# Weights, low weights and activations put at other places in the on-chip memory, and another order in the mixers' matmul triples

## The chip, the cores and the metric

The kernel runs on one core of a Trainium2 chip. The metric is the device time of one execution in microseconds (us). Data is worked on in an on-chip memory of 128 partitions; a tile of shape [128, n] of 4-byte numbers takes 4n bytes of each partition, and its place is the byte in the partition at which it starts.

## The reference

Two blocks of a network on x of 256 tokens by 1024 features. The first block has two layers (a convolution mixer, then neighbourhood attention over x and a context of 256 tokens), the second two layers (a gated linear-attention mixer A, then a sliding-window attention mixer B, each with heads that read a memory of 256 tokens), with gated feed-forward networks (FFNs) before and behind each mixer. Cut to the parts that cost most:

```
def _swiglu(h, w_in, w_out):
    gate, up = jnp.split(h @ w_in, 2, axis=-1)
    return (jax.nn.silu(gate) * up) @ w_out

# first block, each layer
h = _modulate(_rms_norm(x, norm_mix[i]), sh1, sc1)
y = mixer(h)                    # convolution, or attention
x = x + g1 * y
x = x + g2 * _swiglu(_modulate(_rms_norm(x, norm_ffn[i]), sh2, sc2), ffn_w_in[i], ffn_w_out[i])
# second block, each layer
x = x + 0.5 * swiglu(rms_norm(x, ffn1_norm_g[i]), ffn1_w_in[i], ffn1_w_out[i])
proj = rms_norm(x, mix_norm_g[i]) @ w_in
x = x + concatenate([heads(proj), memory_heads(proj)]) @ w_out
x = x + 0.5 * swiglu(rms_norm(x, ffn2_norm_g[i]), ffn2_w_in[i], ffn2_w_out[i])
```

The features are 1024, the hidden width of an FFN 2816, all in 32-bit floats.

## The kernel before

Everything is kept transposed: features in the partitions (8 blocks of 128), tokens along the row. To keep precision in TensorE's fast 32-bit format, each number is split into a high part and a low part (its rest), and a product of two numbers is three matmuls: high by high, high by low, low by high.

Weights come from memory through `WeightStream`: SP's queue loads units of 1024 columns into `wraw` (five buffers), ScalarE copies the high part to `whi` (line 106), VectorE subtracts to get `wlo` (line 107), four buffers each, two units ahead of their use. The order of the units is written out by hand in `stream_specs`.

A matmul has an operand that is loaded into TensorE beforehand (its own LDWEIGHTS instruction; I say "the loaded operand") and one that is streamed through it (the moving operand), 256 or 512 columns wide. There are these forms:

- `mm3` (lines 246 to 248): a triple for one block of 128 features. `wstat` loads weights and streams activations; `xstat` and `xstat_steps` load activations and stream weights. In a triple the loaded operands are high, high, low and the moving ones high, low, high. The convolution and the first FFN's input stream 512 columns (x beside the context), nearly all else 256.
- `pair_unit` (lines 309 and 311), used by `ffn_pairs` for the five other FFNs: the activations' high plane and low plane lie side by side in `x2` (or `s2`, the hidden layer), so one matmul of 512 columns with the high weights does two products; the low weights then take the high plane alone, 256 columns. Four (at unit ends two) of the first kind are followed by as many of the second. `pg` is the accumulator of an FFN's input half, `po` that of its output half.

The order of the work around is that of the program; in attention and the mixers two strands are woven by estimated costs (`weave`).

Where a tile lies follows from the sizes of the tiles opened before it, pool by pool from the left end of the partition, and from the right end for a few. Nothing else sets it: several tiles of before have no use but to shift others (`fill3` to `fill11`, the argument `shift` of `ffn2`, the odd lengths and offsets in `x_tiles`, `net.xc` and `net.xa`).

Of the kernel before, what the change touches and what calls it, by code (L numbers as in the profile page):

```python
# [7 lines left out]
F32 = mybir.dt.float32  # L8
F32R = mybir.dt.float32r
# [6 lines left out]
P = 128  # L16
D = 1024
KB = D // P
T = 256
# [47 lines left out]
class WeightStream:  # L67
# [4 lines left out]
    def __init__(self, net, es, specs, raw_bufs, split_bufs, ahead):  # L72
        self.nc = net.nc
        self.specs = specs
        self.ahead = ahead
        self.raw_bufs = raw_bufs
        self.raw_pool = es.enter_context(net.tc.tile_pool(name="wraw", bufs=raw_bufs))
        self.split_pool = es.enter_context(net.tc.tile_pool(name="wsplit", bufs=split_bufs))
        self.loaded = 0
        self.split = 0  # L80
        self.used = 0
        self.raw = []
        self.ready = []
        self.width = 512
# [9 lines left out]
    def _split(self):  # L94
        self.load(self.split + self.raw_bufs)
        raw, nk, ncol = self.raw.pop(0)
        n = nk * ncol
        v = lambda t: t[:, :n].rearrange("p (k c) -> p k c", k=nk)
        if self.specs[self.split][3]:
            self.ready.append((v(raw), None, nk, ncol))  # L100
        else:
            hi = self.split_pool.tile([P, self.UNIT], F32R, name="whi", tag="hi")
            lo = self.split_pool.tile([P, self.UNIT], F32R, name="wlo", tag="lo")
# [58 lines left out]
class Net:  # L162
    def __init__(self, tc, a, out, es):
        self.tc = tc
        self.nc = tc.nc
        self.a = a
        self.out = out
        self.es = es
        nc = self.nc
# [23 lines left out]
    def x_tiles(self):  # L193

        return [self.xp.tile([P, KB * 512 + n], F32R, name=name, tag=name) for name, n in (("xh", 48), ("xl", 80))]

# [47 lines left out]
    def mm3(self, ps, ah, al, bh, bl, first, last):  # L244
        mm = self.nc.tensor.matmul
        mm(ps, ah, bh, start=first, stop=False)  # L246
        mm(ps, ah, bl, start=False, stop=False)  # L247
        mm(ps, al, bh, start=False, stop=last)  # L248
# [24 lines left out]

    def wstat(self, pss, xh, xl, kblocks):

        done = 0
        while done < len(kblocks):
            unit = self.ws.take()
            self.wstat_unit(unit, pss, xh, xl, kblocks, done)
            done += unit[2]  # L280

    def wstat_unit(self, unit, pss, xh, xl, kblocks, done):
# [32 lines left out]

    def xstat(self, bank, xh, xl):
        for _ in self.xstat_steps(bank, range(2), xh, xl, self.take2()):
            pass

    def partial(self, kblocks, yh, yl, evac, bank=None):  # L320
# [447 lines left out]
def conv_block(net):  # L768
# [134 lines left out]
    with tc.tile_pool(name="hid0", bufs=1) as hp, tc.tile_pool(name="ada", bufs=2) as net.adap:  # L903
        sh = hp.tile([P, 12, 512], F32R, name="sh")
        sl = hp.tile([P, 12, 512], F32R, name="sl")
        evict(0, 2)
# [120 lines left out]
def attention_block(net):  # L1027
# [6 lines left out]
    with ExitStack() as es:  # L1034
        op = es.enter_context(tc.tile_pool(name="attn1", bufs=1))
        heads_pool = es.enter_context(ExitStack())
        ap = heads_pool.enter_context(tc.tile_pool(name="attn", bufs=2))
        oh = op.tile([P, 8, T], F32R, name="oh")
        ol = op.tile([P, 8, T], F32R, name="ol")
        NBIAS = 4  # L1040
# [7 lines left out]
        for i in range(NBIAS - 1):  # L1048
            load_bias(i)
        gq = op.tile([P, P], F32, name="gq")[:, :1]  # L1050
        nc.vector.tensor_scalar(gq, net.p("at_q"), 0.125, None, ALU.mult)
# [124 lines left out]
        for q4 in range(3):  # L1176
            weave(project(q4 + 1), attend(q4), RATIO_ATT)
        x2, m2 = (t[:, o : o + KB * 512].rearrange("p (k a t) -> p k a t", k=KB, a=2) for t, o in zip(net.x_tiles(), (0, 80)))
        mh, ml = m2[:, :, 0, :], m2[:, :, 1, :]
# [32 lines left out]
    for _ in values:  # L1212
        pass
    with tc.tile_pool(name="hid1", bufs=1, reuse_waits="tile") as hp:
        g1 = net.p("ffn1_g0")
        st = {"acc": None}
# [58 lines left out]

def ffn2(net, x2, acc, gain, first, shift, last=False, rope=False):

# [3 lines left out]
    with tc.tile_pool(name="hid", bufs=1) as hp:  # L1281
        if rope:
            rope_tables(net, hp)
        hp.tile([P, shift // 4], F32, name="fill9")

# [13 lines left out]
def memory_query(net, layer, xh, xl, yh, yl, rc):  # L1299
# [6 lines left out]
    for g in range(2):  # L1306
        banks = [net.main_bank()[:, :T] for _ in range(2)]
        net.wstat(banks, xh, xl, list(range(8)))
        for c in range(2):
# [110 lines left out]
def mixer_a(net, x2, acc, gain):  # L1420
# [4 lines left out]
    with tc.tile_pool(name="mixa", bufs=1) as mp:  # L1425
        mp.tile([P, 96], F32, name="fill10")
        yh = mp.tile([P, 12, T], F32R, name="yh")
        yl = mp.tile([P, 12, T], F32R, name="yl")
        mp.tile([P, 32], F32, name="fill11")
        flags = set()  # L1430
# [71 lines left out]
        with tc.tile_pool(name="mixm", bufs=1) as mm:  # L1502
# [10 lines left out]
            def project():  # L1513
# [3 lines left out]
                for h in range(4):  # L1517
                    while h >= 2 and 2 * (h - 2) + 1 not in done:
                        yield WAIT
                    if h % 2 == 0:  # L1520
                        for which in range(2):
                            banks = [net.main_bank()[:, :T] for _ in range(2)]
                            net.wstat(banks, xh, xl, k8)
                            for c in range(2):
# [5 lines left out]
                    bank = net.main_bank()  # L1530
                    net.xstat(bank, xh, xl)
                    vh, vl = vts[h % 2]
# [5 lines left out]
                    bank = net.main_bank()  # L1538
                    net.xstat(bank, xh, xl)
                    og = mp.tile([P, 2, T], F32, name="og", tag="og", bufs=2)  # L1540
# [124 lines left out]
def mixer_b(net, x2, acc, gain):  # L1665
# [3 lines left out]
    with tc.tile_pool(name="mixb", bufs=1) as mp:  # L1669
        mp.tile([P, 64], F32, name="fill10")  # L1670
        yh = mp.tile([P, 12, T], F32R, name="yh")
        yl = mp.tile([P, 12, T], F32R, name="yl")
        mp.tile([P, 64], F32, name="fill11")
        flags = set()
# [49 lines left out]
        with tc.tile_pool(name="mixm", bufs=1) as mm:  # L1724
# [9 lines left out]
            def project():  # L1734
                bank = net.main_bank()
                net.xstat(bank, xh, xl)
                kv = bank.rearrange("p (t c) -> p t c", t=2)
# [30 lines left out]
                for pair in range(2):  # L1768
                    banks = []
                    for i in range(2):  # L1770
                        banks.append(net.main_bank())
                        net.xstat(banks[i], xh, xl)
                        if i == 0:
# [91 lines left out]
def network(tc, a, out, es):  # L1865
    net = Net(tc, a, out, es)
    nc = net.nc
    net.ws = WeightStream(net, es, stream_specs(a), 5, 4, 2)
    net.mk = net.cp.tile([P, 4, T], F32, name="mk")


    net.cp.tile([P, 16], F32, name="fill1")
    es.enter_context(tc.tile_pool(name="top", bufs=1, side="right")).tile([P, 40], F32, name="fill3")
    es.enter_context(tc.tile_pool(name="shift", bufs=1)).tile([P, 80], F32, name="fill4")
# [15 lines left out]
    def next_x():  # L1890
        return net.xp2.tile([P, KB, 2, T], F32R, name="x2", tag="x2")

# [3 lines left out]
    net.rope = net.cp.tile([P, 32], F32, name="rope")  # L1896
    x2, acc = ffn2(net, x2, acc, net.p("mix_g0"), 1, 256, rope=True)
    x2, acc = mixer_a(net, x2, acc, net.p("ffn2_g0"))
    x2, acc = ffn2(net, x2, acc, net.p("ffn1_g1"), 0, 320)
    x2, acc = ffn2(net, x2, acc, net.p("mix_g1"), 1, 384)  # L1900
    x2, acc = mixer_b(net, x2, acc, net.p("ffn2_g1"))
    ffn2(net, x2, acc, None, 0, 128, last=True)

# [110 lines left out]
```

## Time and profile before

| | |
|---|---|
| median of 3 runs | 2021.09 us (2020.64 to 2021.78) |
| the profiled execution | 2022.05 us, of which the span is 2020.3 us |
| TensorE matmuls (PE) | 1997.8 us busy, 12454 instructions |
| weight loads (PEld, beside PE) | 1767.4 us, 12454 |
| VectorE (DVE) | 1496.8 us |
| ScalarE (ACT) | 1025.5 us |
| granted TensorE clock, mean | 0.997 |
| read from memory | 345.68 MB, 172 GB/s over the span |

A row of a group reads: line, engine, operation, out<-in, shapes, count | busy us, mean ns of one | idle time before. A row of the timeline reads: start in us, duration in us, engine, line, operation, count. Durations of matmuls overlap; the step from start to start is shorter than a duration.

### The profile page before, as it was taken

How to read it: one execution, taken by the hardware profiler on the slowest of the kernel's cores; microseconds unless marked ns; L12 is line 12 of the kernel's file. 1: busy time of each engine (PE TensorE's matmuls, PEld its weight loads, DVE VectorE, ACT ScalarE, POOL GpSimd, SP SyncE). 2: the span in 40 equal slices, each digit the busy share in tenths (PEclk: the TensorE clock that was granted, in tenths of full speed). 3: DMA queues.
4: the chain of work that ended last, by engine and by line, in shares of the span. 5: the costliest groups of instructions: out<-in, count | busy, mean ns of one | idle time of the engine just before them, and what ended most of it. 6: DMA issues, size and time to landing. Idle time of an engine off the chain costs nothing. (4 is left out here: it accounts for less than half of the span.)

```text
span 2020.3 us, 32187 instructions
## 1 busy us (share of the span) xinstructions
PE 1997.8 (99%) x12454; PEld 1767.4 (87%) x12454; DVE 1496.8 (74%) x2626; ACT 1025.5 (51%) x1681; POOL 5.1 (0%) x26
## 2 busy tenths in 40 slices
PE   9999999999999999999999999999999999999999
PEld 6788988888899999888888899998888888989888
DVE  5888777767478779766687667787767776888774
ACT  4433532122355656655455556655545555575552
POOL 0000000000000000000000000000000000000000
PEclk9999999999999999999999999999999999999999
DMA  7765455667354333565666664556656656425654
GB/s 239 229 198 178 125 183 172 194 234 249 116 186 123 90 120 121 167 188 184 192 188 187 189 190 126 156 173 194 184 185 195 188 179 189 135 82 175 187 181 135
DMA packets 319274, 348.84 MB, mean 173 GB/s; under 512 B 12625, under 2 KB 307665, under 8 KB 319121
## 3 DMA queue, kind: packets, MB, share of 16 engines
q1 hardware_dynamic: 319120, 346.78, 55.5%
q8 instruction: 98, 1.61, 0.3%
q14 instruction: 56, 0.45, 0.1%
HBM read 345.68 MB, written 1.05 MB: 172 GB/s over the span
## 5 line engine op out<-in xcount | busy, mean ns | idle before, releaser
L107 DVE TENSOR_TENSOR wlo<-wraw,whi 128x512 fp32r<-128x512 f32 (+1 forms) x777 | 702.4, 918 | 343.7 <-ACT whi L106 337.5
L106 ACT CAST whi<-wraw 128x512 fp32r<-128x512 f32 (+1 forms) x777 | 608.7, 804 | 681.2 <-issue 180.7
L309 PE MATMUL pg<-x,whi 128*128 128x512 f32 x1408 | 383.7, 394 | 0.5 <-DVE x L258 0.4
L309 PEld LDWEIGHTS pg<-x,whi 128*128 128x128 f32 x1408 | 239.3, 188 | 32.9 <-DVE x L258 2.8
L309 PE MATMUL po<-s,whi 128*128 128x512 f32 x880 | 242.8, 394 | 0.0
L311 PEld LDWEIGHTS pg<-x,wlo 128*128 128x128 f32 x1408 | 213.5, 188 | 29.5
L311 PE MATMUL pg<-x,wlo 128*128 128x256 f32 x1408 | 219.8, 278 | 0.0
L246 PE MATMUL pm<-xh,whi 128*128 128x512 f32 (+1 forms) x576 | 217.8, 380 | 0.1
L247 PE MATMUL pm<-xl,whi 128*128 128x512 f32 (+1 forms) x576 | 217.6, 378 | 0.0
L248 PE MATMUL pm<-xh,wlo 128*128 128x512 f32 (+1 forms) x576 | 217.4, 378 | 0.0
L467 DVE SCALAR_TENSOR_TENSOR ada_acc<-wraw,sil,ada_acc 128x1024 f32<-128x1024 f32 x112 | 140.8, 1281 | 37.7 <-DMA wraw<-in_w_ada 37.1
L309 PEld LDWEIGHTS po<-s,whi 128*128 128x128 f32 x880 | 148.0, 188 | 17.2
L311 PEld LDWEIGHTS po<-s,wlo 128*128 128x128 f32 x880 | 136.7, 188 | 21.0
L311 PE MATMUL po<-s,wlo 128*128 128x256 f32 x880 | 140.9, 278 | 0.0
L246 PEld LDWEIGHTS pm<-xh,whi 128*128 128x128 f32 x576 | 108.1, 188 | 21.0 <-ACT xh L254 1.0
L247 PEld LDWEIGHTS pm<-xl,whi 128*128 128x128 f32 x576 | 108.4, 188 | 20.6 <-DVE xl L255 0.9
L248 PEld LDWEIGHTS pm<-xh,wlo 128*128 128x128 f32 x576 | 108.3, 188 | 19.9
L246 PE MATMUL pm<-sh,whi 128*128 128x256 f32 (+1 forms) x352 | 113.4, 322 | 0.0
L248 PE MATMUL pm<-sh,wlo 128*128 128x256 f32 (+1 forms) x352 | 113.1, 321 | 0.0
L247 PE MATMUL pm<-sl,whi 128*128 128x256 f32 (+1 forms) x352 | 112.6, 320 | 0.0
L248 PE MATMUL pm<-whi,xl 128*128 128x256 f32 x352 | 98.2, 279 | 0.0
L309 PE MATMUL pg<-xh,whi 128*128 128x512 f32 x352 | 95.9, 394 | 2.0 <-DVE xh L255 2.0
(442 smaller groups left out, 3398.9 us busy)
## 6 DMA issues: line engine op xcount, KB each, us to landing
wraw<-in_ffn_w_in SPq DMA_DIRECT2D x264, 512.0 KB, 3.5
wraw<-in_ffn_w_out SPq DMA_DIRECT2D x128, 512.0 KB, 3.5
wraw<-in_w_ada SPq DMA_DIRECT2D x96, 512.0 KB, 4.6
wraw<-in_a_w_in SPq DMA_DIRECT2D x28, 512.0 KB, 3.7
wraw<-in_attn_w_qkv SPq DMA_DIRECT2D x24, 512.0 KB, 4.2
wraw<-in_conv_w_in SPq DMA_DIRECT2D x18, 512.0 KB, 3.9
wraw<-in_ffn_w_out SPq DMA_DIRECT2D x28, 256.0 KB, 2.8
wraw<-in_b_w_in SPq DMA_DIRECT2D x14, 512.0 KB, 3.7
```

What stands on the lines that cost most here:

```text
L106: self.nc.scalar.copy(hi[:, cs], raw[:, cs])
L107: self.nc.vector.tensor_tensor(lo[:, cs], raw[:, cs], hi[:, cs].bitcast(F32), ALU.subtract)
L246: mm(ps, ah, bh, start=first, stop=False)
L247: mm(ps, ah, bl, start=False, stop=False)
L248: mm(ps, al, bh, start=False, stop=last)
L309: self.nc.tensor.matmul(pss[c], hi[:, kk, cs], x2[:, done + kk], start=done + kk == 0, stop=False)
L311: self.nc.tensor.matmul(pss[c][:, 0, :], lo[:, kk, cs], x2[:, done + kk, 0, :], start=False, stop=done + kk == nblocks - 1)
L467: nc.vector.scalar_tensor_tensor(accs[v], w, c, accs[v], ALU.mult, ALU.add)
```

## The change

Tiles get other places; the order within a triple is turned for some matmuls; the work is the same. The high weights and low weights have pools of their own with 64 bytes between; the fills of before go, and fills of 64 bytes ("16" numbers) stand between high and low activations; `x2` gets planes of T + 16 numbers, so that its low plane starts 1088 bytes behind the high one and a block takes 2176 bytes. With `low_first`, used in the mixers' projections, the moving operands of a triple come low, high, high (the loaded ones stay high, high, low).

The places, as bytes modulo 256, added up from the sizes of the tiles:

| tile | before | after |
|---|---|---|
| whi, wlo | 0, 0 | 0, 64 |
| convolution and first FFN: xh, xl | 0, 0 | 128, 192 |
| first FFN, hidden: sh, sl | 64, 64 | 192, 0 |
| attention: xh, xl | 64, 64 | 64, 128 |
| attention's result: oh, ol | 64, 64 | 192, 0 |
| attention's FFN: x2 (both planes); s2 | 64; 64 | 128; 0 |
| other FFNs and mixers: x2, high plane | 64 | 128 and 0 in turn, block by block |
| the same, low plane | 64 | 192 and 64 in turn |
| the four ffn2: s2 | 64, 128, 192, 192 | 128 in all |
| mixers: yh, yl | A 64, 64; B 192, 192 | 64, 128 |

The diff, cut:

```
         self.raw_pool = es.enter_context(net.tc.tile_pool(name="wraw", bufs=raw_bufs))
-        self.split_pool = es.enter_context(net.tc.tile_pool(name="wsplit", bufs=split_bufs))
+
+        self.hi_pool = es.enter_context(net.tc.tile_pool(name="whi", bufs=split_bufs))
+        es.enter_context(net.tc.tile_pool(name="between", bufs=1)).tile([P, 16], F32, name="fill4")
+        self.lo_pool = es.enter_context(net.tc.tile_pool(name="wlo", bufs=split_bufs))
...
-        return [self.xp.tile([P, KB * 512 + n], F32R, name=name, tag=name) for name, n in (("xh", 48), ("xl", 80))]
+        return [self.xp.tile([P, KB * 512 + 16], F32R, name=name, tag=name) for name in ("xh", "xl")]
...
     def mm3(self, ps, ah, al, bh, bl, first, last):
         mm = self.nc.tensor.matmul
-        mm(ps, ah, bh, start=first, stop=False)
-        mm(ps, ah, bl, start=False, stop=False)
+        mm(ps, ah, bl if self.low_first else bh, start=first, stop=False)
+        mm(ps, ah, bh if self.low_first else bl, start=False, stop=False)
         mm(ps, al, bh, start=False, stop=last)
...
         sh = hp.tile([P, 12, 512], F32R, name="sh")
+        hp.tile([P, 16], F32, name="fill12")
         sl = hp.tile([P, 12, 512], F32R, name="sl")
...
         oh = op.tile([P, 8, T], F32R, name="oh")
+        op.tile([P, 16], F32, name="fill13")
         ol = op.tile([P, 8, T], F32R, name="ol")
...
-def ffn2(net, x2, acc, gain, first, shift, last=False, rope=False):
+def ffn2(net, x2, acc, gain, first, last=False, rope=False):
...
-        hp.tile([P, shift // 4], F32, name="fill9")
+        hp.tile([P, 16], F32, name="fill9")
...
         banks = [net.main_bank()[:, :T] for _ in range(2)]
-        net.wstat(banks, xh, xl, list(range(8)))
+        net.wstat(banks, xh, xl, list(range(8)), True)
...
-        mp.tile([P, 96], F32, name="fill10")
         yh = mp.tile([P, 12, T], F32R, name="yh")
+        mp.tile([P, 16], F32, name="fill10")
         yl = mp.tile([P, 12, T], F32R, name="yl")
-        mp.tile([P, 32], F32, name="fill11")
+        mp.tile([P, 16], F32, name="fill11")
...
                     bank = net.main_bank()
-                    net.xstat(bank, xh, xl)
+                    net.xstat(bank, xh, xl, True)
...
-    net.xc, net.xa = ([t[:, o : o + KB * 512].rearrange("p (k t) -> p k t", k=KB) for t, o in zip(xs, offs)] for offs in ((48, 0), (0, 80)))
+    net.xc, net.xa = ([t[:, o : o + KB * 512].rearrange("p (k t) -> p k t", k=KB) for t, o in zip(xs, offs)] for offs in ((16, 16), (0, 0)))
...
-        return net.xp2.tile([P, KB, 2, T], F32R, name="x2", tag="x2")
+        return net.xp2.tile([P, KB, 2, T + 16], F32R, name="x2", tag="x2")[:, :, :, :T]
```

More of the change, by code (lines that the diff above doesn't have):

```diff
@@ L101, in _split @@
         else:
-            hi = self.split_pool.tile([P, self.UNIT], F32R, name="whi", tag="hi")
-            lo = self.split_pool.tile([P, self.UNIT], F32R, name="wlo", tag="lo")
+            hi = self.hi_pool.tile([P, self.UNIT], F32R, name="whi", tag="hi")
+            lo = self.lo_pool.tile([P, self.UNIT], F32R, name="wlo", tag="lo")
             for c0 in range(0, n, self.width):
@@ L168, in __init__ @@
         self.es = es
+        self.low_first = False
         nc = self.nc
@@ L272, in newton, with wstat @@
             nc.vector.scalar_tensor_tensor(y if i == 2 else g, t, 1.5, g, ALU.add, ALU.mult)
-    def wstat(self, pss, xh, xl, kblocks):
+    def wstat(self, pss, xh, xl, kblocks, low_first=False):
+        self.low_first = low_first
         done = 0
@@ L280, in wstat @@
             done += unit[2]
+        self.low_first = False
     def wstat_unit(self, unit, pss, xh, xl, kblocks, done):
@@ L314, in take2, with xstat @@
         return [self.ws.take(), self.ws.take()]
-    def xstat(self, bank, xh, xl):
+    def xstat(self, bank, xh, xl, low_first=False):
+        self.low_first = low_first
         for _ in self.xstat_steps(bank, range(2), xh, xl, self.take2()):
             pass
+        self.low_first = False
     def partial(self, kblocks, yh, yl, evac, bank=None):
@@ L1049, in attention_block @@
             load_bias(i)
-        gq = op.tile([P, P], F32, name="gq")[:, :1]
+        gq = op.tile([P, 112], F32, name="gq")[:, :1]
         nc.vector.tensor_scalar(gq, net.p("at_q"), 0.125, None, ALU.mult)
@@ L1177, in attention_block @@
             weave(project(q4 + 1), attend(q4), RATIO_ATT)
-        x2, m2 = (t[:, o : o + KB * 512].rearrange("p (k a t) -> p k a t", k=KB, a=2) for t, o in zip(net.x_tiles(), (0, 80)))
+        x2, m2 = (t[:, o : o + KB * 512].rearrange("p (k a t) -> p k a t", k=KB, a=2) for t, o in zip(net.x_tiles(), (16, 16)))
         mh, ml = m2[:, :, 0, :], m2[:, :, 1, :]
@@ L1283, in ffn2 @@
             rope_tables(net, hp)
-        hp.tile([P, shift // 4], F32, name="fill9")
+        hp.tile([P, 16], F32, name="fill9")
         def evac(kb, ps):
@@ L1522, in project @@
                             banks = [net.main_bank()[:, :T] for _ in range(2)]
-                            net.wstat(banks, xh, xl, k8)
+                            net.wstat(banks, xh, xl, k8, True)
                             for c in range(2):
@@ L1538, in project @@
                     bank = net.main_bank()
-                    net.xstat(bank, xh, xl)
+                    net.xstat(bank, xh, xl, True)
                     og = mp.tile([P, 2, T], F32, name="og", tag="og", bufs=2)
@@ L1669, in mixer_b @@
     with tc.tile_pool(name="mixb", bufs=1) as mp:
-        mp.tile([P, 64], F32, name="fill10")
         yh = mp.tile([P, 12, T], F32R, name="yh")
+        mp.tile([P, 16], F32, name="fill10")
         yl = mp.tile([P, 12, T], F32R, name="yl")
-        mp.tile([P, 64], F32, name="fill11")
+        mp.tile([P, 16], F32, name="fill11")
         flags = set()
@@ L1735, in project @@
                 bank = net.main_bank()
-                net.xstat(bank, xh, xl)
+                net.xstat(bank, xh, xl, True)
                 kv = bank.rearrange("p (t c) -> p t c", t=2)
@@ L1771, in project @@
                         banks.append(net.main_bank())
-                        net.xstat(banks[i], xh, xl)
+                        net.xstat(banks[i], xh, xl, True)
                         if i == 0:
@@ L1867, in network @@
     nc = net.nc
+    net.cp.tile([P, 16], F32, name="fill1")
     net.ws = WeightStream(net, es, stream_specs(a), 5, 4, 2)
     net.mk = net.cp.tile([P, 4, T], F32, name="mk")
-    net.cp.tile([P, 16], F32, name="fill1")
-    es.enter_context(tc.tile_pool(name="top", bufs=1, side="right")).tile([P, 40], F32, name="fill3")
-    es.enter_context(tc.tile_pool(name="shift", bufs=1)).tile([P, 80], F32, name="fill4")
+    es.enter_context(tc.tile_pool(name="top", bufs=1, side="right")).tile([P, 24], F32, name="fill3")
     net.x_pool = es.enter_context(ExitStack())
@@ L1896, in network @@
     net.rope = net.cp.tile([P, 32], F32, name="rope")
-    x2, acc = ffn2(net, x2, acc, net.p("mix_g0"), 1, 256, rope=True)
+    x2, acc = ffn2(net, x2, acc, net.p("mix_g0"), 1, rope=True)
     x2, acc = mixer_a(net, x2, acc, net.p("ffn2_g0"))
-    x2, acc = ffn2(net, x2, acc, net.p("ffn1_g1"), 0, 320)
-    x2, acc = ffn2(net, x2, acc, net.p("mix_g1"), 1, 384)
+    x2, acc = ffn2(net, x2, acc, net.p("ffn1_g1"), 0)
+    x2, acc = ffn2(net, x2, acc, net.p("mix_g1"), 1)
     x2, acc = mixer_b(net, x2, acc, net.p("ffn2_g1"))
-    ffn2(net, x2, acc, None, 0, 128, last=True)
+    ffn2(net, x2, acc, None, 0, last=True)
 def host_arrays(inputs):
```

## The prediction

> **What bounds the kernel now.** First the page: is one engine full, and at full clock?
>
> ```profile
> span 2020.3 us, 32187 instructions
> PE 1997.8 (99%) x12454; PEld 1767.4 (87%) x12454; DVE 1496.8 (74%) x2626; ACT 1025.5 (51%) x1681; POOL 5.1 (0%) x26
> PEclk9999999999999999999999999999999999999999
> PE 32%; DVE 3%; ACT 1%; issue 1%
> ```
>
> TensorE is busy in 99% of the span in all 40 slices and leads the chain. The list of what it waited for comes next; its longest entry is
>
> ```profile
> PE pa L1073 <- DVE t L1023: 2.4, 2, 1.2
> ```
>
> 2.4 us, and no entry names whi or wlo. So no transfer and no split is late: the time is the pace at which matmuls follow one another, and the change does nothing but move their operands. Next, therefore, the groups of instructions with shapes kept apart (count | busy us, mean ns of one):
>
> ```profile
> L309 PE MATMUL pg<-x,whi 128*128 128x512 f32 x1408 | 383.7, 394 | 0.5 <-DVE x L258 0.4
> L309 PE MATMUL po<-s,whi 128*128 128x512 f32 x880 | 242.8, 394 | 0.0
> L309 PE MATMUL pg<-xh,whi 128*128 128x512 f32 x352 | 95.9, 394 | 2.0 <-DVE xh L255 2.0
> L311 PE MATMUL pg<-x,wlo 128*128 128x256 f32 x1408 | 219.8, 278 | 0.0
> L246 PE MATMUL pm<-xh,whi 128*128 128x512 f32 x512 | 200.0, 392 | 0.1
> L248 PE MATMUL pm<-sh,wlo 128*128 128x512 f32 x128 | 50.4, 394 | 0.0
> L248 PE MATMUL pm<-whi,xl 128*128 128x256 f32 x352 | 98.2, 279 | 0.0
> L247 PE MATMUL pm<-wlo,x 128*128 128x256 f32 x208 | 58.4, 281 | 0.0
> L247 PE MATMUL pm<-x,whi 128*128 128x256 f32 x128 | 35.7, 279 | 0.0
> ```
>
> One shape takes 392 or 394, 278 or 281 ns. A duration here is longer than the step to the next start (they overlap), but the two differ by a constant, so a difference of durations is a difference of pace. What tells the groups apart is place. While one matmul streams its moving operand, the next one's weights are loaded, as the timeline of the load shows (the row starts 0.01 us after the matmul of 1735.09 below):
>
> ```profile
> 1735.10 0.19 PEld L247 LDWEIGHTS pm<-wlo,x 128*128 128x128 f32 x1
> ```
>
> I call a matmul "level" when its moving operand and the operand loaded next start at the same byte modulo 128, and "apart" when they are 64 off (both from the table of places). Three stretches of 256-column matmuls, timeline, first and last rows:
>
> ```profile
> 1735.09 0.28 PE L246 MATMUL pm<-whi,x 128*128 128x256 f32 x1
> ...
> 1736.79 0.28 PE L246 MATMUL pm<-whi,x 128*128 128x256 f32 x1
> 1713.72 0.28 PE L248 MATMUL pm<-x,wlo 128*128 128x256 f32 x1
> ...
> 1716.90 0.28 PE L248 MATMUL pm<-x,wlo 128*128 128x256 f32 x1
> 246.73 0.28 PE L246 MATMUL pm<-xh,whi 128*128 128x256 f32 x1
> ...
> 247.93 0.28 PE L247 MATMUL pm<-xl,whi 128*128 128x256 f32 x1
> ```
>
> 15 steps in 1.70 us: 113 ns, apart. 27 steps in 3.18 us: 118 ns, also apart. 10 steps in 1.20 us: 120 ns, level. So apart is not one price: it has a "settled" pace (113) and an "unsettled" one (118), and each holds for long stretches. The same in 512 columns, where the convolution runs level, just after eight transposes have disturbed it:
>
> ```profile
> 153.34 0.40 PE L247 MATMUL pm<-xl,whi 128*128 128x512 f32 x1
> ...
> 155.42 0.39 PE L247 MATMUL pm<-xl,whi 128*128 128x512 f32 x1
> ...
> 157.46 0.39 PE L247 MATMUL pm<-xl,whi 128*128 128x512 f32 x1
> ```
>
> Nine steps in 2.08 us (231.1 ns), then nine in 2.04 us (226.7 ns), and it stays there: a level 512 stream settles, but needs nine undisturbed matmuls for it. Last, the page's best experiment: the output half of the second ffn2, whose s2 lies level, against that of the first, whose s2 lies apart (groups in the windows 1142 to 1202 and 1468.5 to 1529 us, the apart one first):
>
> ```profile
> L309 PE MATMUL po<-s,whi 128*128 128x512 f32 x164 | 45.1, 393 | 0.0
> L311 PE MATMUL po<-s,wlo 128*128 128x256 f32 x164 | 26.2, 278 | 0.0
> L309 PE MATMUL po<-s,whi 128*128 128x512 f32 x164 | 45.6, 396 | 0.0
> L311 PE MATMUL po<-s,wlo 128*128 128x256 f32 x164 | 26.7, 280 | 0.0
> ```
>
> Level is slower there for the 512s too, by 3 ns: the runs of four 512s between four 256s are shorter than the nine it needs to settle.
>
> In every stream of before all moving operands share one place modulo 256 (table). The settled paces occur in such streams only, and before has no other kind. I read settling as a matter of the starts falling into step with that one place.
>
> **The change part by part.**
>
> No instruction, transfer or byte is added; the fill tiles issue nothing, and the queues of SP and POOL keep their order. Two things differ: places, and the order in a triple.
>
> 1. *FFN pairs, 512 columns* (2640: the first three rows of groups). x2 and s2 go to a multiple of 128, as the high weights: three of four become level, the fourth (low weights next) stays apart. Row: level in this very pattern, +3 ns. 1980 x 3 = +5.9 us. Lower end: the settled level pace, 389 ns, the row
>
> ```profile
> L247 PE MATMUL pm<-xl,whi 128*128 128x512 f32 x65 | 25.3, 389 | 0.0
> ```
>
> (the first FFN's input, 300 to 345 us): 1980 x -4 = -7.9 us. Upper: +3 on all, +7.9. I take the FFN's own row, since it is the same pattern of fours.
>
> 2. *FFN pairs, 256 columns* (2640). Three of four stay apart (low weights 64 on, x level with a multiple of 128), the fourth, before a high load, becomes level. In x2 the plane of T+16 makes a block 2176 bytes, so the place modulo 256 alternates from block to block: nothing to settle on. I take +1 on the three (between 278 and 281) and +2 on the fourth (280): 1980 + 1320 ns = +3.3 us. Ends: settled at 276 throughout, 1980 x -2 = -4.0 us; unsettled with the fourth at the level price below, 1980 x 2 + 660 x 8 = +9.2 us.
>
> ```profile
> L248 PE MATMUL pm<-xh,wlo 128*128 128x256 f32 x55 | 15.5, 286 | 0.0
> L247 PE MATMUL pm<-wlo,x 128*128 128x256 f32 x33 | 9.1, 276 | 0.0
> ```
>
> (The first is the level stretch of the first FFN, 229 to 255 us; the second the settled one in the second mixer, 1728 to 1740 us.) The 64-byte gap inside a 512-column operand of x2 has no row: between the paces 226.7 and 231.1 it could be 4.4 ns either way on 1408, 6.2 us; I take 0, as the gap is passed in the second half, when the 0.19 us load is nearly over.
>
> 3. *Convolution and first FFN's input, 512 columns* (3 x 512). Level before and after modulo 128, but a triple now moves hi, lo, hi at places 64 apart modulo 256, and xh lies 128 from the weights modulo 256, as in the slower output half, not 0. I take the loss of the settled pace: 231.1 - 226.7 = 4.4 ns x 1536 = +6.8 us. Ends: 0, and the 396 of the level FFN, +7 x 1536 = +10.8.
>
> 4. *Attention's projections* (3 x 352 with the memory's): apart stays apart, but the weights alternate by 64 between high and low. 279 to 281: +2.1 us; ends -3 x 1056 = -3.2 (276) and +2.1.
>
> 5. *Mixers with the low part first* (3 x 208 with x loaded, 3 x 128 with x streamed). x2's high plane is now level with the high weights. In the new order two of three are apart, the third level; in the old order all three would be level. Third at 286, others as before: 1008/3 x 6 = +2.0 us, and +1 for the two others, 0.7. Ends 0 and 1008 x 6 = 6.0. The new order asks for wlo one matmul earlier: VectorE's split must be done 0.113 us sooner, for 26 units at most 2.9 us, and PE's queue would stand behind it; I take 0, because PE's list of waits has no wlo at all (units are split two ahead).
>
> 6. *sh, oh, yh with their low parts* (3 x 128 of 512 columns, 3 x 256 of 256 columns):
>
> ```profile
> L248 PE MATMUL pm<-yh,wlo 128*128 128x256 f32 x128 | 35.9, 281 | 0.0
> L248 PE MATMUL pa<-yh,wlo 128*128 128x256 f32 x64 | 17.9, 280 | 0.0
> L248 PE MATMUL pm<-oh,wlo 128*128 128x256 f32 x64 | 18.0, 282 | 0.0
> ```
>
> Apart remains, alternating: +2 and +1 ns, +1.5 us; ends -2 x 768 = -1.5 and +3.5.
>
> Sum: 5.9 + 3.3 + 6.8 + 2.1 + 2.7 + 1.5 = +22.3 us. The profiled execution took 2022.05 us, 0.96 above the median of 2021.09 shown; from the median that is 2043.4.
>
> A rule speaks against all of this. The Trainium skill, "SBUF — State Buffer", section "SBUF: two separate sides", says that only the port pair shared by VectorE and GpSimd contends, and that PE never waits on anyone; "TensorE: Matmul & The Clock Gate", Part 2, adds that loading the next weights takes no read bandwidth from the running matmul, which has a port of its own. By that, place could not matter and the sum would be 0. The trace disagrees: 276 against 286 ns for one shape.
>
> **The rivals.**
>
> *The modulo-128 rule is the whole story (faster).* Then a level 512 runs at 389 everywhere, an apart 256 at 276, and only the level 256s pay. FFN: -7.9 - 4.0 + 660 x 8 = -6.6 us; attention -3.2; mixers +2.0, streams -1.5: -9 us, 2012. For it: the settled rows 389 and 276 exist, the latter in the second mixer with 64 between operands. Against it: the level output half at 396. It decides if a 512 in the FFN falls below 391.
>
> *Place does nothing here, or gains and losses cancel (no change).* Each group is already a mixture of settled and unsettled, and a new mixture may average the same: 278 lies between 276 and 281. 2021. This is also the figure by which the skill's rule would come out. Against it: the 2640 + 1536 + 1056 matmuls of terms 1, 3 and 4 change class or lose their common place.
>
> **How the numbers follow.** Slower as summed: 0.64, as term 1 has a row in the very pattern but that row's 256s were level too. Faster by the modulo-128 rule: 0.22, since after parts those 256s. No change: 0.14. A difference under 0.2%, 4 us, can't be told from none, and the cases fall on either side of it as they stand. All upper ends together are 7.9 + 9.2 + 6.2 + 10.8 + 2.1 + 6.0 + 2.9 + 3.5 = 48.6, all lower ones -7.9 - 4.0 - 6.2 - 3.2 - 1.5 = -22.8; they won't all come on one side, so the forecast's own range goes half of the way to each: 22.3 + 13 and 22.3 - 18 (under that it is no longer slower by 0.2%), 2025 to 2056. To leave out no more than 2 in 10 the lower end goes down past no change to the faster rival's 2012, less 2.
>
> **What would show it.** In the profile after: the convolution's 512s at 392 to 396 instead of 389, with no long stretch of 226.7 ns steps; L309 at 395 to 397; L311 at 279 to 281; the third of a mixer triple (L248) above the two others; PE's idle time and its waits unchanged. The prediction is wrong if a stream whose places alternate still settles, since terms 3, 4 and 6 rest on that alone, or if level 512s in the FFN pairs, now beside settled 256s, fall into step after all.

## The result, and the profile after

The changed kernel takes 2044.2 us (median of 4 runs, 2042.6 to 2044.45) against 2021.26 us (2020.64 to 2021.78) before: ratio 1.0115, 95% interval 1.0103 to 1.0128. It is slower by 23 us; the forecast was 22.

The page of the changed kernel, and the longest entry of TensorE's list of waits:

```profile
span 2040.8 us, 32187 instructions
PE 2021.1 (99%) x12454; PEld 1779.6 (87%) x12454; DVE 1497.5 (73%) x2626; ACT 1026.1 (50%) x1681; POOL 5.1 (0%) x26
PE pa L1083 <- DVE t L1032: 2.0, 2, 1.0
```

The counts are those of before, the mean granted clock is 0.998 (0.997 before), VectorE and ScalarE are as busy as they were, and no wait has come up: wlo is nowhere in the list though the mixers now ask for it one matmul sooner. TensorE alone is busy 23.3 us longer. Its idle time (span less busy time) fell from 22.5 to 19.7 us, so the profiled span is 20.5 us longer: the profile of before is of an execution above its median, that of after of the fastest of four. Its groups of instructions (columns as in the prediction; lines 309, 311, 246 to 248 are now 315, 317, 250 to 252):

```profile
L315 PE MATMUL pg<-x,whi 128*128 128x512 f32 x1408 | 386.3, 395 | 0.5 <-DVE x L262 0.4
L315 PE MATMUL po<-s,whi 128*128 128x512 f32 x880 | 244.2, 395 | 0.0
L315 PE MATMUL pg<-xh,whi 128*128 128x512 f32 x352 | 98.1, 400 | 1.9 <-DVE xh L259 1.9
L317 PE MATMUL pg<-x,wlo 128*128 128x256 f32 x1408 | 223.0, 280 | 0.0
L317 PE MATMUL po<-s,wlo 128*128 128x256 f32 x880 | 143.6, 281 | 0.0
L317 PE MATMUL pg<-xh,wlo 128*128 128x256 f32 x352 | 56.4, 282 | 0.0
L250 PE MATMUL pm<-xh,whi 128*128 128x512 f32 x512 | 201.6, 395 | 0.0
L251 PE MATMUL pm<-xl,whi 128*128 128x512 f32 x512 | 201.3, 393 | 0.0
L252 PE MATMUL pm<-xh,wlo 128*128 128x512 f32 x512 | 203.2, 397 | 0.0
L252 PE MATMUL pm<-whi,xl 128*128 128x256 f32 x352 | 99.1, 282 | 0.0
L252 PE MATMUL pm<-whi,x 128*128 128x256 f32 x208 | 58.9, 283 | 0.0
...
L441 PE MATMUL pa<-wraw,sil 128*2 128x256 f32 x64 | 14.6, 379 | 0.0
```

Every FFN group is 1 to 6 ns a matmul longer. So is the convolution (3 to 8 ns), which has lost its settled stretch (timeline, 12 steps in 2.79 us, 232.5 ns):

```profile
169.72 0.39 PE L250 MATMUL pm<-xh,whi 128*128 128x512 f32 x1
...
172.51 0.39 PE L250 MATMUL pm<-xh,whi 128*128 128x512 f32 x1
```

By the forecast's terms, from the busy times of after less before (a difference of durations is one of pace):

| term | rows | forecast | measured |
|---|---|---|---|
| 1 FFN 512s | +2.6 +1.4 +2.2 | 5.9 | 6.2 |
| 2 FFN 256s | +3.2 +2.7 +1.4 | 3.3 | 7.3 |
| 3 convolution, first FFN's input | +1.6 +1.8 +3.8 | 6.8 | 7.2 |
| 4 attention's projections | | 2.1 | 2.7 |
| 5 mixers | x loaded +0.3, x streamed +0.3 | 2.7 | 0.6 |
| 6 sh, oh, yh | | 1.5 | 3.4 |

Together +27.4. Against it stand -1.7 on the last row above (16.3 to 14.6), -1.0 on the matmuls of means with ones (L788 before) and -1.4 on groups too small for a term.

Part of these differences is the clock and not the change. In both profiles the granted clock falls to half for a few stretches of 3.4 us; each costs TensorE some 1.7 us, and they fall on other rows from one execution to the next. Before has four of them while TensorE works, at 14, 1212, 1724 and 1782 us, after has two, at 841 and 1801 us. Two stretches of before, then two of after (a row reads: stretch in us, its length, TensorE's busy time and count, granted clock, busy share of DMA, GB/s):

```profile
14.10:17.50 3.40, 3.40 (x9) 0.51 0.61 212
1724.20:1727.60 3.40, 3.40 (x19) 0.50 0.56 155
14.10:17.50 3.40, 3.40 (x17) 1.00 0.91 303
841.40:844.80 3.40, 3.20 (x10) 0.50 0.00 0
```

The one at 14 us lies on the last row of the groups, and is its -1.7; in b_conv128 below, which has none there and whose edit doesn't touch that row, it also takes 14.6 us. The one at 1212 us lies on a small group of mixer A (24 matmuls, -1.8 us). Two of them distort terms. That of after at 841 us lies on the input half of attention's FFN; the run a_nolow below, which has the same places there and no such stretch, gives for it

```profile
L315 PE MATMUL pg<-xh,whi 128*128 128x512 f32 x352 | 97.0, 397 | 2.0 <-DVE xh L259 2.0
L317 PE MATMUL pg<-xh,wlo 128*128 128x256 f32 x352 | 55.7, 279 | 0.0
```

so that term 1 is 5.1 and term 2 is 6.6 us. That of before at 1724 us lies on the mixers' rows with x loaded; the run best1 below, which has the places of before in these rows and no such stretch, takes 58.1, 58.0 and 58.3 us for them instead of 58.5, 58.4 and 58.7, so that term 5 is 1.8 us. The terms then add up to 26.8 us.

The size is right. What remains to be shown is whether the reasons are.

### The profile page after: what moved, and what is told of

It is laid out like the page before. It is cut to its first block, busy times and chain, and to the rows that moved or that the text cites. A ratio compares the mean times of both kernels' runs of the same rounds, so it can differ in the third digit from the quotient of the medians.

```text
span 2040.8 us, 32187 instructions
## 1 busy us (share of the span) xinstructions
PE 2021.1 (99%) x12454; PEld 1779.6 (87%) x12454; DVE 1497.5 (73%) x2626; ACT 1026.1 (50%) x1681; POOL 5.1 (0%) x26
```

## The experiments

Theory A is the prediction's: a stream settles if all its moving operands share one place modulo 256; within that, level or apart (modulo 128) sets the price. Rival B: level or apart alone. Rival C was formed on the changed kernel's trace, where groups of four 512s and four 256s repeat exactly. Timeline, start of the four 512s of a group; first and eighth group of a stretch, before (x2 of the second ffn2) and after (the same stretch, then s2 behind it):

```profile
1358.77 1.09 PE L309 MATMUL pg<-x,whi 128*128 128x512 f32 x4
...
1368.45 1.07 PE L309 MATMUL pg<-x,whi 128*128 128x512 f32 x4
```

```profile
1374.40 1.09 PE L315 MATMUL pg<-x,whi 128*128 128x512 f32 x4
...
1384.20 1.09 PE L315 MATMUL pg<-x,whi 128*128 128x512 f32 x4
...
1497.65 1.10 PE L315 MATMUL po<-s,whi 128*128 128x512 f32 x4
...
1507.54 1.10 PE L315 MATMUL po<-s,whi 128*128 128x512 f32 x4
```

Seven groups: 9.68, 9.80 and 9.89 us, that is 1383, 1400 and 1413 ns. Counted in units of 1/2.4 ns (called a cycle here), these are 3320, 3360 and 3392 cycles, or 207.5, 210 and 212 times 16. So rival C: each set of places falls into a repeating pattern of its own, over one or a few groups, whose length is some multiple of 16 cycles.

**probe: matmuls alone.** No code of the network; a loop like this for many places, on zeros:

```
+ for kk in range(4): matmul(bank,  hi[kk], x[kk] (512 columns))
+ for kk in range(4): matmul(bank,  lo[kk], x[kk] (256 columns))
```

> This kernel computes none of the reference: it issues only matmuls, on zeros, from chosen places: FFN groups (four of 512 columns with the high weights, four of 256 with the low) 12 times each for 16 pairs of places (moving operand at 0, 64, 128, 192 bytes modulo 256, high weights at 0, low weights at 0, 64, 128, 192), twice over; groups with gaps between the planes; triples of 512 and 256 columns for 64 sets of places each. By starts, the two kernels gave for a group: activations 64, low weights 0: 1383 ns; 128, 0: 1405; 128, 64: 1413; 0, 64: 1400; alternating 128 and 0, 64: 1400. Theory A (the prediction's: one common place settles, alternating places do not): triples whose two moving places are equal run at 226.7 or 113 ns, others at 231 or 118. Rival B (only level or apart modulo 128 counts): moving places 0 and 128 are alike, 64 and 192 alike, and groups with low weights at 64 beat those with 0 where the activations are at 0 or 128. Rival C (each set of places falls into a repeating pattern of its own, a whole multiple of 16 cycles, 6.67 ns, long): group times are multiples of 6.67 ns over one or a few groups, the four places all differ, and some sets beat 1383 ns while neighbours 64 bytes on do not. If the surroundings (VectorE, ScalarE, transfers) made the pattern, the probe would not repeat the five group times named.

With VectorE, ScalarE and the queues idle, four of the five group times named are repeated. The fifth (activations at 128, low weights at 64) comes out at 3376 cycles instead of 3392, 1407 ns instead of 1413; in the changed kernel these places run at both, as the last experiments show. Timeline of the probe, eight groups apart, with activations at 64 and then at 128 (low weights at 0):

```profile
81.56 1.09 PE L1893 MATMUL pg<-q 128*128 128x512 f32 x4
...
92.63 1.09 PE L1893 MATMUL pg<-q 128*128 128x512 f32 x4
...
147.60 1.09 PE L1893 MATMUL pg<-q 128*128 128x512 f32 x4
...
158.83 1.10 PE L1893 MATMUL pg<-q 128*128 128x512 f32 x4
```

1384 and 1404 ns. All 16 sets, mean cycles of a group, from the starts:

```
activations at   low weights at 0     64    128    192
  0                         3368   3360   3376   3376
 64                         3320   3328   3376   3360
128                         3373   3376   3384   3328
192                         3328   3360   3344   3344
```

0 and 128 differ, 64 and 192 differ: rival B is out. Common place throughout, and still no order: theory A is out as well. The kernel before has the best of the sixteen; with the changed kernel's gaps and alternation the probe gives 3360, as the kernel. Streams of 36 show two places that settle. Triples of 512 columns with everything at 0, then with the activations at 128; triples of 256 with moving operands at 64, then at 192 (loaded ones at 0); duration of all 36:

```profile
1091.44 8.43 PE L1904 MATMUL pg<-q 128*128 128x512 f32 x36
...
1175.51 8.61 PE L1904 MATMUL pg<-q 128*128 128x512 f32 x36
...
1653.88 4.48 PE L1904 MATMUL pg<-q 128*128 128x256 f32 x36
...
1697.60 4.35 PE L1904 MATMUL pg<-q 128*128 128x256 f32 x36
```

Once settled, 544 against 558 cycles and 283 against 272. So the settled pace of 512s belongs to operands level modulo 256 (here all at 0, the one such set), not 128: of the 63 other sets of 512-column triples none runs at 544; the nearest stand at 549. A 256-column triple runs at 272 in three of the 64 sets: moving operands at 192 with the low weights at 0 or at 128, and moving operands at 64 with the low weights at 128. With all weights at 0, 192 ahead settles and 64 ahead doesn't, which is also what sets apart the two "apart" stretches of the prediction (at 1735 us weights at 0 move over an x at 64, at 1714 us x at 64 moves over weights at 0); the third set shows that this is no rule for every set.

**b_conv128 and b_wlo64: one part of the change done alone**, on the kernel before.

```
b_conv128
- for name, n in (("xh", 48), ("xl", 80))          + (("xh", 80), ("xl", 48))
- for offs in ((48, 0), (0, 80))                   + ((80, 0), (0, 48))
b_wlo64
- lo = self.split_pool.tile(...)                   + lo = self.lo_pool.tile(...)   # 64 bytes behind
```

> The kernel before with one edit: the convolution's and the first FFN's input xh and xl both lie at 128 bytes modulo 256 instead of 0; nothing else moves. Theory A (one common place settles): as before, 2021 us, the 512-column steps of the convolution at 226.7 ns. The prediction's second reason for its third term (128 bytes away from the weights modulo 256 is slower, as in the level output half): +5 to +8 us, 2026 to 2029, with steps of 231 to 234 ns. Rival B (modulo 128 only): as before, 2021.

> The kernel before with one edit: the low weights in a pool of their own, 64 bytes behind modulo 256; all activations stay. Theory A: the FFNs' 256-column matmuls (activations 64, next load 64) become level, three of four: 2640 x 0.75 x 4.5 ns = +9 us, and attention's and the mixers' moving weights alternate: about +3; 2033 us. Rival B: the same FFN loss, nothing for alternation: 2030. Rival C (patterns of a whole group): no forecast for the sign; a group time that is a multiple of 6.67 ns, other than 1383. If place did nothing: 2021.

b_conv128: 2027.48 us, before 2019.94, ratio 1.0044 (1.0030 to 1.0058). b_wlo64: 2034.05, ratio 1.0075 (1.0062 to 1.0088). Groups of the two:

```profile
L246 PE MATMUL pm<-xh,whi 128*128 128x512 f32 x512 | 202.7, 397 | 0.5 <-ACT xh L254 0.5
L247 PE MATMUL pm<-xl,whi 128*128 128x512 f32 x512 | 202.0, 395 | 0.0
L248 PE MATMUL pm<-xh,wlo 128*128 128x512 f32 x512 | 202.0, 395 | 0.0
L433 PE MATMUL pa<-wraw,sil 128*2 128x256 f32 x64 | 14.6, 379 | 0.0
```

```profile
L248 PE MATMUL pm<-xh,whi 128*128 128x512 f32 x512 | 200.1, 392 | 0.8 <-ACT xh L256 0.8
L249 PE MATMUL pm<-xl,whi 128*128 128x512 f32 x512 | 200.8, 393 | 0.0
L250 PE MATMUL pm<-xh,wlo 128*128 128x512 f32 x512 | 203.2, 397 | 0.0
L311 PE MATMUL pg<-x,whi 128*128 128x512 f32 x1408 | 381.0, 392 | 0.5 <-DVE x L260 0.4
L313 PE MATMUL pg<-x,wlo 128*128 128x256 f32 x1408 | 223.7, 282 | 0.0
```

In the first one common place, level modulo 128, costs the convolution 7.8 us by its rows: theory A is wrong there, its second reason right. In the second the convolution's own tiles haven't moved and it loses 5.2 us all the same, because the low weights left 0. The total, 2034, is the one that theory A gave, but from other places: it had the FFNs down for +9, and there the 512s fell by 2.7 us while the 256s rose by 3.9. Of the 512s one in four (the one before a low load) had changed class, to level, which the prediction priced as slower, and the row got faster. So the class of a single matmul doesn't set its pace; the pattern of the whole group fits.

**a_nolow, a_conv128, a_nopad, a_wlo0: one part undone**, on the changed kernel.

```
a_nolow
- mm(ps, ah, bl if self.low_first else bh, ...)    + mm(ps, ah, bh, ...)      # and bl second
a_conv128
- for offs in ((16, 16), (0, 0))                   + ((16, 0), (0, 0))
a_nopad
- xp2.tile([P, KB, 2, T + 16])[:, :, :, :T]        + xp2.tile([P, KB, 2, T])
a_wlo0
- the 16 numbers between whi and wlo               + the same behind wlo
```

> The changed kernel with one edit: the mixers' triples keep the old order (high, low, high); all places as changed. The prediction's fifth term: two more matmuls of each of 336 triples become level, 672 x 6 ns = +4 us, 2048. Rival: the order costs and gains nothing, since VectorE's splits are two units ahead and the mixers' matmuls are unsettled in either order: 2044. If the earlier need of wlo cost something: 2041 to 2043.

> The changed kernel with one edit: the low part of the convolution's and first FFN's input lies at 128 modulo 256 as the high part, instead of 192. So the moving places no longer alternate. Theory A (the prediction's third term: alternating places cost the settled pace): the 7.6 us that the convolution and the first FFN's input lost come back, 2036.5. Theory C with the first probe's rows (triples with moving 128, 192, 128 and low weights at 64: 557.3 cycles a matmul; with 128, 128, 128: 559.6): 1536 x 2.3 cycles = +1.5 us, 2045.

> The changed kernel with one edit: x2's planes have T numbers instead of T + 16, so the place no longer alternates from block to block and both planes lie at 128 modulo 256. Theory A (one common place settles, level 512s and apart 256s): the four FFNs with x2 come under 1383 ns a group: 352 groups x 17 ns or more, -6 us, 2038. Theory C with the first probe's rows (128, 0, 64: 3376 cycles; with the gap and alternating: 3360, as in the changed kernel): 352 x 6.7 ns = +2.3 us in the FFNs, and in the mixers (streamed triples, low first, 128 throughout with low weights at 64: 281 cycles against 282; loaded ones within 1 %) about nothing: 2046.

> The changed kernel with one edit: the low weights back at 0 modulo 256, as the high ones; everything else as changed. Prediction's classes (rival B too): the FFNs' 256-column matmuls turn from apart to level, 1980 x 8 ns = +16 us, 2060. Theory C with the probes' rows: convolution 557.3 to 554.6 cycles, -1.7 us; s2 at 128 and 0: 3376 to 3373 and 3360 to 3368 cycles, nothing; the alternating x2 with low weights at 0 wasn't probed (352 groups, 7 ns for each step of 16 cycles); all within 5 us of 2044.

| run | us | ratio to before, interval |
|---|---|---|
| changed kernel | 2044.2 | 1.0115, 1.0103 to 1.0128 |
| a_nolow | 2043.18 | 1.0123, 1.0108 to 1.0138 |
| a_conv128 | 2046.43 | 1.0127, 1.0112 to 1.0141 |
| a_nopad | 2049.62 | 1.0140, 1.0124 to 1.0155 |
| a_wlo0 | 2043.73 | 1.0115, 1.0099 to 1.0131 |

The order in the triple can't be told from nothing (the mixers' rows rise by 0.9 us, where the prediction's classes gave 4). Taking the alternation out of the convolution gives nothing back (rows +1.8 us, rival C +1.5), taking it out of x2 makes the FFNs slower:

```profile
L315 PE MATMUL pg<-x,whi 128*128 128x512 f32 x1408 | 388.3, 397 | 0.4 <-DVE x L262 0.3
L317 PE MATMUL pg<-x,wlo 128*128 128x256 f32 x1408 | 225.1, 282 | 0.0
```

That is +4.1 us in these rows where theory A had -6 and rival C +2.3; the sign is C's. The interval of this run overlaps the changed kernel's, so the rows carry it, and the groups: those of x2 go from 3360 cycles to 3392 in two of the four ffn2 and to 3376, the probe's figure, in the other two. And turning three of four FFN 256s level (a_wlo0) costs nothing where the prediction's classes gave +16 us: the two rows become 385.8 and 221.9 us. The low weights' 64 bytes cost 14 us on the kernel before and nothing on the changed one. The parts don't add: one step takes the kernel out of its good patterns, and the next finds them gone.

**probe2, best1, best2, best3: looking for better places.**

> Again matmuls alone, none of the reference: FFN groups (four of 512 columns, four of 256), nine for each set of places, high weights at 0: activations and low weights each on all multiples of 16 bytes up to 240, 256 sets; then gaps of 16 to 240 bytes between the planes, with activations at 0, 64, 128, 192 and low weights at 0 or 64. In the first probe the best of 16 sets was the place of the kernel before (64; 0, 0: 3320 cycles of 2.4 GHz, 1383 ns). If every matmul ran at the best step seen in a stream (544 and 272 cycles), a group would take 3264 cycles. Theory C (each set falls into a repeating pattern, whose mean is a multiple of 8 or 16 cycles or a third of it): values between 3264 and 3410 without order by distance, most near 3360, and a few sets under 3320; each cycle less is worth 660/2400 = 0.275 us in the kernel. Rival B (modulo 128): values at x and x + 128 equal.

256 sets on a grid of 16 bytes have a mean of 3363 and a median of 3360 cycles; 7 of them are at 3320 or below, the best is activations 144, low weights 128: 3296. The slowest takes 3456. Sets whose activations are 128 bytes apart don't agree: they differ by 20 cycles in the mean.

```
best1 (on before)
+ 32 numbers ahead of sh, of oh and of mixer B's yh          # place 192
- ffn2 shifts 256, 320, 384, 128                             + 256 in all    # s2 at 64
best2 (on before; oh, ol and mixer B's yh, yl as in best1)
+ lo tile 32 numbers further on for units of pair FFNs       # low weights at 128 there
+ x2 of these FFNs 80 bytes further on, their s2 moved too   # 144
best3 (on best2)
- x2 and its low weights moved                               + only s2 and its low weights
```

> The kernel before with other places for six tiles, chosen from the first probe: sh, sl, oh, ol and mixer B's yh, yl at 192 modulo 256 instead of 64 (256-column triples: 272.0 cycles a matmul instead of 282.7; 512-column ones 560 instead of 549.4), s2 of the last three FFNs at 64 instead of 128, 192, 192 (3320 cycles a group instead of 3373, 3328, 3328). Theory C: -10.7 x (672 + 192 + 288) + 10.6 x 384 - (53 + 8 + 8) x 44 cycles = -4.7 us: 2016. Theory A and rival B (192 and 64 are alike, apart and common): only the s2 of the second, -1 us: 2020.

> The kernel before with places from the second probe: in the FFNs with pairs, x2 and s2 lie at 144 modulo 256 and the low weights at 128 (group of 3296 cycles in the probe), while attention and mixers keep their x at 64 and low weights at 0; oh, ol and mixer B's yh, yl at 192 as in the run before this one, sh and sl back at 64. Theory C: 660 groups x 24 cycles = -6.6 us in the FFNs, -1 us from s2 of the last three against the kernel before, and +0.9 us that sh and sl at 192 had cost (512 columns +1.6, 256 columns -0.7) is not paid: 2019.8 - 8 = 2012. Rival: a place has more than one pattern, and the entry in the kernel (groups of two at unit ends, transposes between) sets another than the probe's: FFN groups at 3360 cycles, +11 us, 2031. Theory A: common places throughout, weights 16 to 144 away: no settled pace by modulo 64, no forecast below 2020.

> The kernel of the run with x2 and s2 at 144, with one edit: x2 goes back to 64 and its low weights to 0; only s2 stays at 144 with low weights at 128. In that run the groups of s2 ran in the probe's pattern (1374 ns), those of x2 in a slower one (1386 against 1383 ns in the kernel before), for the same places. Theory C with the two-pattern rival joined to it: s2 keeps 1374 ns, x2 returns to 1383, so the 1.9 us that x2 and the first pair FFN had lost there come back: 3 + 1.9 = 4.8 us under the kernel before of the same chip, about 2015. If s2's pattern hangs on the phase that x2's groups hand over, s2 falls into another (1387 ns or more): 2018 or above. If neither: the places of x2 make no difference and it stays 2017.6.

best1: 2017.02 us, ratio 0.9987 (0.9979 to 0.9996). best2: 2017.63, 0.9986 (0.9977 to 0.9995). best3: 2016.60, 0.9989 (0.9980 to 0.9998). All three beat the kernel before, by 0.1%, which is not the 8 us that the probe promised best2. Its timeline says why: eight groups of x2, then twice eight of s2, all with the same places (rows of L312 alone).

```profile
1355.78 1.08 PE L312 MATMUL pg<-x,whi 128*128 128x512 f32 x4
...
1365.48 1.08 PE L312 MATMUL pg<-x,whi 128*128 128x512 f32 x4
...
1463.94 1.08 PE L312 MATMUL po<-s,whi 128*128 128x512 f32 x4
...
1473.64 1.08 PE L312 MATMUL po<-s,whi 128*128 128x512 f32 x4
1475.03 0.62 PE L312 MATMUL po<-s,whi 128*128 128x512 f32 x2
...
1477.80 1.08 PE L312 MATMUL po<-s,whi 128*128 128x512 f32 x4
...
1487.42 1.08 PE L312 MATMUL po<-s,whi 128*128 128x512 f32 x4
```

Seven groups in 9.70, 9.70 and 9.62 us: 1386, 1386 and 1374 ns. The places allow two patterns, 3328 and 3296 cycles. Over the four ffn2, whole groups by their starts:

```
             x2 (344 groups)               s2 (160 groups)
before       3320: 330                     3328: 77, 3320: 40, 3376: 14
after        3360: 333                     3392: 80, 3376: 68
best2        3328: 331, 3296: 5            3328: 88, 3296: 72
best3        3320: 332, 3288: 3            3328: 88, 3296: 70
```

A pattern holds from its entry until something breaks the stream. For s2 the trace of best2 shows where: in each ffn2 it runs ten groups at 3328, ten at 3296, ten at 3328 and ten at 3296, and the pattern changes at the shorter groups of two that stand between the tens, as at 1475 us. In the ffn2 of after 3376 and 3392 take turns in the same way. For x2 the place alone doesn't decide either: the input half of attention's FFN, which best2 puts at the same places, ran 85 of its 88 groups at 3296, and its output half then starts at 3296, where that of the ffn2, behind an x2 at 3328, starts at 3328. So the expectation for best3 took too much of s2 at 1374 ns, and the loss on attention's FFN that it counts back was the clock (half at 830 us of best2). best1 also falls short of its probe: in it sh and sl, at the place where the probe's 256s settle (272), stay unsettled (rows 62.8, 62.4 and 62.6 against 63.0, 62.6 and 62.8 before), where settled 256s would have saved 1.0 us a row (224 x 4.5 ns), and their 512s pay for the move (50.7, 50.4, 50.5 against 50.3, 49.9, 50.4). Rival C is right that the place decides which patterns there are; it doesn't say which one is entered. The traces show it handed on from the groups ahead and changed at breaks; an experiment on that wasn't made.

## Why the prediction was right or wrong, point by point

The bound held: the other engines and the transfers did the same work, and what grew is TensorE's own pace. The rival sum of 0 is out: the change costs 23 us, and in the probes, with every other engine idle, place alone moves a group between 3296 and 3456 cycles. The Trainium skill, "SBUF — State Buffer", section "SBUF: two separate sides", says that PE never waits on anyone; the probes don't show TensorE waiting for another engine, but they do show that its pace depends on the places of its own two operands.

*Term 1 (5.9, measured 6.2, or 5.1 without the clock).* The row that it took, the second ffn2's s2 at 128, has the activations' place that the change gives to s2 in all four ffn2, though with the low weights at 0. That is 656 of the 2640 matmuls; the x2 of the ffn2, 1408 more, went to places that alternate, and nothing in before had that pattern. That the row's price came near for the others as well is luck, and the reason given for it, level modulo 128, fell with b_wlo64 and a_wlo0.

*Term 2 (3.3, measured 7.3, or 6.6 without the clock)* was mis-sized. It took the 256s as three unsettled at +1 and a fourth at +2; the rows went up by 2 to 4 ns, as most groups passed from 3320 cycles, in which every second group runs its 256s at 271 to 274 cycles, to 3360 and more, in which none does.

*Term 3 (6.8, measured 7.2).* The loss of the settled pace is right, the cause in the main wrong: not alternation, but that the operands no longer all lie at 0 modulo 256. The reason named second in the same sentence, 128 bytes between x and weights, held: it alone costs 7.8 us (b_conv128), and taking the alternation out gives nothing back (a_conv128). It isn't the only way to lose the pace, as b_wlo64 lost 5.2 us by the low weights alone.

*Terms 4 and 6 (2.1 and 1.5; 2.7 and 3.4)* have the right sign. Term 4 was put down to weights that alternate; with the low weights back at 0 (a_wlo0) its rows still stand 2.1 us above before, so that alone isn't its cause. Term 6 is less than half of what came, because its count leaves out the 3 x 224 matmuls of 256 columns that read sh: they rose by 1.7 us. The table of places ahead of the prediction has the two mixers' yh and yl interchanged: A's were at 192 before, B's at 64. Both are apart, so no term changes by it.

*Term 5 (2.7, measured 0.6, or 1.8 without the clock).* The third matmul of a triple with x loaded went up by 3 ns, from 280 (best1) to 283, not by the 6 that the first FFN's 286 had suggested. The new order costs no wait, as said.

The rival on the other side needed an FFN 512 under 391 ns; the rows are 395 to 400. "No change" came nearest in the mixers.

The sum came out within 1 us partly by luck. Without the clock the terms add up to 26.8 us, 4.5 more than forecast, most of it in terms 2 and 6. Against that, TensorE's idle time, which the prediction took as unchanged, fell by 2.8 us, and the matmuls of means took 1.0 us less, a row that lies between 8.4 and 10.0 us over all profiles. Why the idle time fell stays open. The sign was safe for a reason that the prediction doesn't give: for the FFN groups before stands low in the spread of patterns (3320 among 256 sets with a median of 3360), and a step to nearly any other set costs.

## What to carry to other kernels

Where TensorE is full, compare the steps from start to start of one shape in one repeating group, and take a row of the same pattern over a rule on single operands. A probe that issues nothing but the group, over all places, costs one run and tells which patterns there are; whether the kernel enters the good one has to be read in the kernel. Before a difference of some us between two rows is explained, look up the granted clock in the stretches where they lie. The places of this kernel had been tuned and stood at a low point of a rough surface; with such a kernel, judge a change of several places at once by where the average set lies, and don't add up parts measured alone.

## What the hardware showed that was not expected

- Steps of matmuls fall into repeating patterns: the same eight matmuls take 3296, 3320, 3328, 3360, 3376 or 3392 cycles of 1/2.4 ns in the kernels' long stretches, and 3296 to 3456 over the 256 sets of places of probe2, with every other engine idle.
- One set of places can hold two patterns (3296 and 3328 within one stage of best2, 3376 and 3392 within one of after), and one stage changes from one to the other at a break in the stream.
- Places 128 bytes apart aren't alike, and neither are places 16 bytes apart: 3368 at 0, 3344 at 16, 3360 at 32, 3320 at 64, 3373 at 128 (low weights at 0). Whether places 256 bytes apart are alike wasn't tried.
- Parts of a change of places don't add: the low weights' 64 bytes are worth 14 us on one kernel and 0 on the other.
- The granted clock falls to half for stretches of 3.4 us (0.50 at 1724 us of before), four while TensorE works in one profile, two in the other, at different rows; each is worth some 1.7 us.
